# Stick-breaking attention from cumulated weights and differences of neighbouring value rows

## The chip, the cores and the metric

The kernel runs on one core of one Trainium2 chip. The metric is the device time of one execution, in microseconds (us). A core has five engines with a queue of instructions each: TensorE (PE in the profile; PEld is its loading of weights), VectorE (DVE), ScalarE (ACT), GpSimd (POOL) and SyncE (SP), which here only issues DMAs. Each engine works its queue in order and waits where an instruction's inputs are not there yet. DMAs move data between the device memory (HBM) and the on-chip memory (SBUF, 128 partitions), or within SBUF; their packets run on 16 DMA engines of the core.

## The reference

One sequence of 512 positions with 1024 features goes through two layers, all in float32. Layer 0 is gated linear attention and an MLP. Layer 1 is stick-breaking attention with 16 heads of 64 features, and an MLP; its keys and values come from one projection. The part that the change touches:

```python
z = jnp.einsum('bqhd,bkhd->bhqk', q_blk, k_blk) * scale
mask = s_idx[None, :] < t_idx[:, None]
log_1m = jnp.where(mask, jax.nn.log_sigmoid(-z), 0.0)
rev = lax.cumsum(log_1m, axis=3, reverse=True)
log_w = jax.nn.log_sigmoid(z) + (rev - log_1m)
w = jnp.where(mask, jnp.exp(log_w), 0.0)
outs.append(jnp.einsum('bhqk,bkhd->bqhd', w, v_blk))
```

So a query t gives key s < t the weight sigmoid(z_ts) times the product of (1 - sigmoid(z_tj)) over all keys j between s and t.

## The kernel before, in words

Everything is float32; most matmuls are made of three products of operands that are split into a high and a low part (`split_tile`, lines 67 to 73: ACT makes `hi`, DVE makes `lo`). The order in which each engine runs its instructions is set when the kernel is built: a scheduler orders them from the code's order, and `tc.keep_in_program_order` and `tc.high_priority` bind some of them. Buffers come from rotating pools, and an instruction that reuses a buffer waits until its last reader is done.

The stages are: gated linear attention; MLP 0; the values of layer 1 (`values`, lines 768 to 854, a product of 512x1024 by 1024x1024 made from seven half products); attention; the output projection; MLP 1.

**Values.** The last steps of the layer norm before this stage are transposes of the four 128-row tiles of the hidden state (`turn_affine`, line 231, on PE). Two of these tiles, tiles 2 and 3, are turned between the value matmuls: `late.pop(0)(None)` in lines 809 and 813 stands once after the first `part` (12 matmuls of line 794) and once later. The values end in two tiles `vs[0]` and `vs[1]`, 128 partitions x 4 blocks x 512 floats: row 128 j + p of the values is partition p of block j, and `vs[0]` holds heads 0 to 7, `vs[1]` heads 8 to 15.

**Attention** goes over eight pairs of heads, p = 0 to 7 (line 997). For each p the code does the keys and queries of pair p + 2, in the middle of which the weights of pair p are transposed (`turn`, line 962, on PE, copied out by ACT in line 967); then `weights` of pair p + 1, which begins with its scores (line 925, on PE); then `outputs` of pair p (line 976), 4 steps over the blocks of value rows. The keys are split by `put` (lines 98 and 99: `kh` on ACT, `kl` on DVE), the queries in lines 913 and 914 (`qh`, `ql`). PSUM has 8 banks that are handed out in turn, so the scores of a pair take over a bank that `kl` of the pair after next has to have read.

`weights` handles the two heads in five tiles of 128 x 512 that hold, side by side, the score rows of the blocks of queries: a mask is added on DVE (line 942); ACT makes `r` = sigmoid(-z) and `w` = sigmoid(z) (lines 949 and 950); DVE makes the running product of `r` from the right with one scan over the tile (line 952), in which a tile of zeros and ones, `begin`, restarts it where a segment ends; and the weight is `w` times the scan one column further right (line 953), on POOL for four of the five tiles and on DVE for the fifth.

Weights in device memory reach SBUF through SP's queue: `split_piece` (line 64) loads 512 KB into one of three `raw` buffers, so a load waits on SP until `split_tile` has split the piece three loads earlier, and every DMA behind it on SP's queue waits too. After p = 0 and p = 1 the code has DVE apply the layer norm's gain and bias to a tile of the hidden state (`affine`, line 196, four instructions).

Of the kernel before, what the change touches and what calls it, by code (L numbers as in the profile page):

```python
# [8 lines left out]
F32 = mybir.dt.float32  # L9
F32R = mybir.dt.float32r  # L10
I32 = mybir.dt.int32
AF = mybir.ActivationFunctionType
ALU = mybir.AluOpType

P = 128
S = 512
D = 1024
NT = S // P
# [16 lines left out]
def yoco_kernel(ctx: ExitStack, tc: tile.TileContext, x, gla_w_in, gla_w_a2, gla_b_a, gla_norm_g,  # L35
                gla_w_o, kv_w, sb_w_q, sb_w_o, mlp_w_up, mlp_w_down, ln_g, ln_b, out):
    nc = tc.nc
# [10 lines left out]
    def nm(s):  # L48
        uid[0] += 1
        return f"{s}{uid[0]}"  # L50
# [407 lines left out]
    for u in range(2):  # L458
        for t in range(NT):
            nc.sync.dma_start(out=xs[t][:, 512 * u:512 * u + 512],  # L460
                              in_=x2[128 * t:128 * t + 128, 512 * u:512 * u + 512])
# [4 lines left out]
            k = 4 * u + t  # L466
# [24 lines left out]
    for k in range(8):  # L491
# [6 lines left out]
                                   op1=ALU.subtract)  # L498
    pcs = pieces_512(w_in, 0, 8, 2 * QK + 512)
    for h in range(GH):  # L500
# [3 lines left out]
        c = slice(128 * h, 128 * h + 128)  # L504
# [153 lines left out]
    op = tc.tile_pool(name="gated", bufs=1, reuse_waits="tile")  # L658
# [21 lines left out]
    hs = [Rows() for _ in range(NT)]  # L680
    for t in range(NT):
        nc.sync.dma_start(out=hs[t].h, in_=x2[128 * t:128 * t + 128, :])
    vec, vcols = lnvec(0, 0), lncols(0, 0)
    steps = seven(*onT, lambda k, h, j: block(gla_w_o[0], 512 * k + 256 * h, 512 * j), opp, hs, True, norms=range(NT),
                  mid=lambda: turn_gated(3, 1), ends=True, begun=begun)
    hT = Split()
    late = finish(steps, vcols, hs, hT, sgs)
# [60 lines left out]
    vs = []  # L748
# [19 lines left out]
    def values(y, late, bs):  # L768

        a11, a21, a12, a22 = y[0][:, :, 0:256], y[0][:, :, 256:512], y[1][:, :, 0:256], y[1][:, :, 256:512]  # L770
        whole = lambda u, c0: lambda k, s: tuple(w[u][:, k, c0 + 128 * s:c0 + 128 * s + 128] for w in (h2T.hi, h2T.lo))
        tt = nc.vector.tensor_tensor

        def pieces(bs, keep=lambda ins: ins):
            got = []
            for b in bs:
                hi, lo = split_tile(b, 2, keep)
                got += [(hi[:, i, :], lo[:, i, :]) for i in range(2)]
            return got

        def plain(k, j):
            got = []
            for h in range(2):
                hi, lo = split_piece(v_weights(k, h, j), 2)
                got += [(hi[:, i, :], lo[:, i, :]) for i in range(2)]
            return got

        def part(s, a, b, banks, opens=True, closes=True):

            if opens:  # L790
                banks[s] = bank()
            for k in range(4):
                for x, w in ((0, 0), (0, 1), (1, 0)):
                    nc.tensor.matmul(banks[s], lhsT=a(k, s)[x], rhs=b[k][w],  # L794
                                     start=opens and (k, x, w) == (0, 0, 0),
                                     stop=closes and (k, x, w) == (3, 1, 0), skip_group_check=True)

        def fresh(s, banks, i, j):
            nc.scalar.activation(vs[j][:, 2 * i + s, :], banks[s], AF.Copy, scale=-1.0 if j else 1.0)

        def add(s, banks, i, j):
            v = vs[j][:, 2 * i + s, :]
            tt(v, v, banks[s], op=ALU.subtract if j else ALU.add)

        ys, xs, ws, zs = ([None, None] for _ in range(4))
        b21, b22, b11, b12 = bs
        p1, p2 = plain(0, 0), pieces(b21)
        part(0, whole(0, 0), p1, ys, True, False)
        late.pop(0)(None)
        part(1, whole(0, 0), p1, ys, True, False)  # L810
        part(0, whole(1, 0), p2, xs)
        keys0 = piece_128(kv_w, 0)
        late.pop(0)(None)
        part(1, whole(1, 0), p2, xs)
        more(b12, 0, 0)
        held = [bank(), bank()]
        cols_by(held[0], keys0, 0, 256)
        cols_by(held[0], keys0, 256, 256)
        queries0 = piece_128(sb_w_q[0], 0)
        cols_by(held[1], queries0, 0, 512)  # L820
        for h in range(2):
            tc.keep_in_program_order(tt(b11[h], b22[h], b11[h], op=ALU.add))
            tc.keep_in_program_order(tt(b21[h], b21[h], b11[h], op=ALU.add))
        p4 = pieces(b21, tc.keep_in_program_order)
        vs.extend([unit(F32), unit(F32)])
        tt(a22, a22, a21, op=ALU.subtract)
        p5 = split_a(a22), pieces(b12)
        for s in range(2):
            part(s, whole(1, 256), p4, ws)
        for s in range(2):  # L830
            fresh(s, ys, 0, 0)
            add(s, xs, 0, 0)
        tt(a21, a11, a21, op=ALU.subtract)
        minus = lambda out, a, b: nc.vector.scalar_tensor_tensor(out, a, -1.0, b, op0=ALU.mult, op1=ALU.subtract)
        minus(a11, a22, a11)
        p6 = split_a(a11), pieces(b11)
        for s in range(2):
            part(s, *p5, zs, True, False)
            fresh(s, ws, 1, 0)
            fresh(s, zs, 1, 1)  # L840
        minus(a12, a12, a11)
        p3 = split_a(a12), plain(1, 1)
        for s in range(2):
            part(s, *p6, ys, False, False)
            fresh(s, ys, 0, 1)
        p7 = split_a(a21), pieces(b22)
        for s in range(2):
            part(s, *p3, zs, False, True)
            add(s, zs, 0, 1)
        for s in range(2):  # L850
            part(s, *p7, ys, False, True)
            add(s, ys, 1, 1)
            add(s, ys, 1, 0)
        return held
# [24 lines left out]
    sbp = sbx.__enter__()  # L879
# [3 lines left out]

    low = tri(sbp, "low", F32, 0.0, -1.0e30, [[-1, P]], ALU.is_gt, 1)

    begin = sbp.tile([P, 6 * P], F32, name="begin")
    nc.gpsimd.memset(begin, 0.0)
    nc.gpsimd.memset(begin[:, 511:512], 1.0)
    begins = (begin[:, 0:512], begin[:, 128:640], begin[:, 256:768])

    def chain():
        return sbp.tile([P, S], F32, tag="w", bufs=6, name=nm("w"))

    HALVES = ((A0, A1), (A1, A0))

    class Pair:
# [5 lines left out]
        def part(self, tag):  # L902
            return sbp.tile([P, S], F32R, tag=tag, bufs=2, name=nm(tag))
# [26 lines left out]
        def weights(self):  # L930

            self.ws = []
            zs = self.scores()
            for kind, segs, banks in ((0, ((0, 3, 0),), (0,)), (0, ((1, 3, 0),), (1,)), (1, ((0, 2, 0), (0, 0, 384)), (2,)),
                                      (1, ((1, 2, 0), (1, 0, 384)), (3,)), (2, ((0, 1, 0), (1, 1, 256)), (4, 5))):
                n = S // len(banks)
                views = [(slice(n * i, n * i + n), zs[b][:, n * i:n * i + n]) for i, b in enumerate(banks)]

                for _, z in views:
                    z4 = z.rearrange("p (b c) -> p b c", c=P)  # L940
                    last = z4[:, (slice(3, 4), slice(2, 4), slice(1, 2))[kind], :]
                    nc.vector.tensor_tensor(last, last, low.unsqueeze(1).broadcast_to([P, last.shape[1], P]),
                                            op=ALU.add)
                r = sbp.tile([P, S + 1], F32, tag="r", bufs=3, name=nm("r"))
                w = chain()
                nc.gpsimd.memset(r[:, S:S + 1], 1.0)
                rb = r[:, 0:S]
                for at, z in views:
                    nc.scalar.activation(rb[:, at], z, AF.Sigmoid, scale=-1.0)  # L949
                    nc.scalar.activation(w[:, at], z, AF.Sigmoid)  # L950
                down = rb[:, ::-1]
                nc.vector.tensor_tensor_scan(down, down, begins[kind][:, ::-1], 1.0, op0=ALU.mult, op1=ALU.max)  # L952
                (nc.vector if kind == 2 else nc.gpsimd).tensor_tensor(w, w, r[:, 1:S + 1], op=ALU.mult)  # L953
                self.ws.append((segs, w))

        def turn(self):

# [31 lines left out]
    vec, vcols = lnvec(0, 1), lncols(1, 0)  # L989
# [3 lines left out]
        h.affine(vec, tc.keep_in_program_order)  # L993
    pairs[1].keys()
    pairs[0].weights()
    pairs[1].queries()
    for p in range(NP):
        if p + 2 < NP:
            pairs[p + 2].keys()
            made = pairs[p].turn()  # L1000
            pairs[p + 2].queries(lambda k: [next(made, None) for _ in range(TAKE.get(k, 0))])
        else:
            n = p - (NP - 2)
            pcs = pieces_512(sb_w_o[0], 0, 4, 512 * n)
            made = pairs[p].turn()
            for t in range(NT):
                hs[t].add(n, rows(oA, t, pcs, range(4)), True)
                for _ in range(((0, 1, 2, 2), (1, 1, 2, 1))[n][t]):
                    next(made, None)
        if p + 1 < NP:  # L1010
            pairs[p + 1].weights()
        if p < 2:
            hs[2 + p].affine(vec, tc.keep_in_program_order)
        if p in (4, 6):
            u = unit(F32R)
            parts += [(u[:, i, :], u[:, 2 + i, :]) for i in range(2)]
        pairs[p].outputs(*parts[p], LAST if p == NP - 1 else [(j, j, NT) for j in range(NT)])
# [88 lines left out]
```

## Time and profile before

| | us |
|---|---|
| median of 3 runs | 1117.32 |
| fastest run | 1117.02 |
| the profiled execution | 1117.43 |
| its span, first instruction to last | 1115.7 |
| PE busy in it | 1106.8 (99%) |
| DVE busy | 828.4 (74%) |
| ACT busy | 559.7 (50%) |
| POOL busy | 175.1 (16%) |

The span is what the profile's pages and times refer to; 1.7 us of the execution lie around it. An engine that is busy most of the span does not set the time by that alone: what matters is whose waiting ends last in a stage. A row of the list of groups gives line, engine, operation, output and inputs, shape and count, then the busy time and the mean duration. A row of the timeline gives start, duration and what the instruction is, and in brackets how long its engine was idle before it and which engine and line ended that.

### The profile page before, as it was taken

Reading aid. Unit: us, or ns where it says so; the run is one execution under the profiler, and the core shown is the slowest. Engines: PE = TensorE matmul, PEld = TensorE weight load, DVE = VectorE, ACT = ScalarE, POOL = GpSimd, SP = SyncE. Lnnn points to the kernel's source line nnn. Section 1 sums busy time; section 2 is a strip of 40 time slices with the busy share of each in tenths; the row PEclk is TensorE's granted clock in tenths of the full one; section 3 lists DMA queues with packets and bytes.
Section 4 is the critical chain, followed back from the end, with each engine's and each line's share of the span. In section 5 each row is a group of like instructions: output and inputs, shape, how many; then the busy total and the mean of one; then the engine's idle time right before and its main releaser. Section 6 shows DMA issues by size and latency. Waiting matters only on the chain.

```text
span 1115.7 us, 14408 instructions
## 1 busy us (share of the span) xinstructions
PE 1106.8 (99%) x5515; PEld 917.2 (82%) x5515; DVE 828.4 (74%) x993; ACT 559.7 (50%) x839; POOL 175.1 (16%) x217
## 2 busy tenths in 40 slices
PE   9999999999999999999999999999999999999998
PEld 7888888898888888888788777778988888888886
DVE  4677639957966856858899898887389767667677
ACT  4455437653533534536675666665445435336363
POOL 1011222200100100122301324330200000001132
PEclk9999999999999999999999999999999999999999
DMA  8441399392670770797743331211946816706774
GB/s 249 122 133 57 105 262 211 126 299 95 188 207 21 202 208 22 197 203 151 226 91 113 95 114 43 72 42 55 292 112 196 240 47 169 227 19 189 170 132 94
DMA packets 107544, 161.72 MB, mean 145 GB/s; under 512 B 12434, under 2 KB 37394, under 8 KB 107476
## 3 DMA queue, kind: packets, MB, share of 16 engines
q1 hardware_dynamic: 85684, 118.34, 32.6%
q0 software_dynamic: 19328, 37.75, 19.7%
q10 hardware_dynamic: 2464, 4.72, 1.2%
q8 instruction: 43, 0.70, 0.2%
q14 instruction: 25, 0.20, 0.1%
HBM read 157.64 MB, written 3.15 MB: 144 GB/s over the span
## 4 chain that ended last, share of the span: by engine, by line
PE 96%; DVE 2%; issue 1%; POOL 0%; ACT 0%; POOLq 0%; DVEq 0%; ACTq 0%
PE ps L355 29%; PE ps L93 19%; PE ps L94 19%; PE ps L95 19%; PE ps L794 3%; PE ps L976 2%; PE ps L925 2%; PE ps L962 2%; PE ps L231 1%; DVE lo L72 1%; PE ps L584 0%; DVE h L169 0%; PE ps L121 0%; DVE bst L177 0%; DVE T L99 0%
## 5 line engine op out<-in xcount | busy, mean ns | idle before, releaser
L355 PE MATMUL ps<-hi,T 128*128 128x512 f32 x1008 | 313.4, 390 | 0.1
L93 PE MATMUL ps<-T,hi 128*128 128x512 f32 (+1 forms) x776 | 290.3, 374 | 0.0
L94 PE MATMUL ps<-T,hi 128*128 128x512 f32 (+1 forms) x776 | 287.2, 370 | 0.1
L95 PE MATMUL ps<-T,lo 128*128 128x512 f32 (+1 forms) x776 | 287.0, 370 | 0.0
L72 DVE TENSOR_TENSOR lo<-raw,hi 128x1024 fp32r<-128x1024 f32 x130 | 158.5, 1224 | 98.5 <-ACT hi L70 94.8
L355 PEld LDWEIGHTS ps<-hi,T 128*128 128x128 f32 x1008 | 188.9, 188 | 40.1 <-DVE T L99 0.6
L70 ACT ACTIVATE hi<-raw 128x1024 fp32r<-128x1024 f32 x130 | 137.8, 1064 | 163.2 <-PE ps L355 58.8
L70 ACT ACTIVATE hi<-B 128x1024 fp32r<-128x1024 f32 x118 | 124.4, 1059 | 169.7 <-PE ps L94 104.0
L72 DVE TENSOR_TENSOR lo<-B,hi 128x1024 fp32r<-128x1024 f32 x118 | 142.9, 1221 | 83.9 <-ACT hi L70 83.8
L355 PE MATMUL ps<-lo,T 128*128 128x512 f32 x504 | 196.2, 389 | 0.0
L95 PEld LDWEIGHTS ps<-T,lo 128*128 128x128 f32 x776 | 146.3, 189 | 25.0
L93 PEld LDWEIGHTS ps<-T,hi 128*128 128x128 f32 x776 | 146.2, 189 | 24.3 <-issue 0.7
L94 PEld LDWEIGHTS ps<-T,hi 128*128 128x128 f32 x776 | 146.4, 189 | 23.8 <-DVE T L99 0.4
L314 POOL DMA_DIRECT2D B<-in_mlp_w_down_dram x52 | 62.9, 1257 | 544.0 <-DMA B<-in_mlp_w_down_dram 378.5
L355 PEld LDWEIGHTS ps<-lo,T 128*128 128x128 f32 x504 | 94.6, 188 | 19.5
L169 DVE TENSOR_TENSOR h<-h,ps 128x512 f32<-128x512 f32 x110 | 74.8, 682 | 6.9 <-PE ps L95 4.0
L93 PE MATMUL ps<-hi,T 128*128 128x512 f32 x192 | 77.4, 403 | 0.0
L95 PE MATMUL ps<-hi,T 128*128 128x512 f32 x192 | 75.3, 392 | 0.0
L94 PE MATMUL ps<-lo,T 128*128 128x512 f32 x192 | 75.1, 391 | 0.0
L952 DVE TENSOR_TENSOR_SCAN r<-r,begin 128x512 f32<-128x512 f32 x40 | 65.8, 1650 | 2.8 <-ACT r L949 2.8
L953 POOL TENSOR_TENSOR w<-w,r 128x512 f32<-128x512 f32 x32 | 51.9, 1624 | 94.5 <-DVE r L952 68.2
L99 DVE TENSOR_TENSOR T<-s,T 128x1024 fp32r<-128x1024 f32 (+1 forms) x50 | 53.4, 1069 | 10.6 <-ACT T L98 10.6
(190 smaller groups left out, 1243.4 us busy)
## 6 DMA issues: line engine op xcount, KB each, us to landing
raw<-in_mlp_w_up_dram SPq DMA_DIRECT2D x64, 512.0 KB, 5.6
B<-in_mlp_w_down_dram SPq DMA_DIRECT2D x64, 512.0 KB, 5.3
B<-in_mlp_w_down_dram POOLq DMA_DIRECT2D x52, 512.0 KB, 8.0
raw<-in_gla_w_in_dram SPq DMA_DIRECT2D x20, 512.0 KB, 3.6
raw<-in_mlp_w_down_dram SPq DMA_DIRECT2D x16, 512.0 KB, 4.4
B<-in_gla_w_o_dram POOLq DMA_DIRECT2D x14, 512.0 KB, 8.5
raw<-in_kv_w_dram SPq DMA_DIRECT2D x12, 512.0 KB, 4.5
B<-in_gla_w_o_dram SPq DMA_DIRECT2D x8, 512.0 KB, 6.2
```

Of the source, the lines that this page charges most:

```text
L70: keep(nc.scalar.activation(hi, raw, AF.Copy))
L72: keep(nc.vector.tensor_tensor(lo, raw, hi.bitcast(F32), op=ALU.subtract))
L93: keep(nc.tensor.matmul(ps, lhsT=a[0], rhs=b[0], start=first, stop=False))
L94: keep(nc.tensor.matmul(ps, lhsT=a[0], rhs=b[1], start=False, stop=False))
L95: keep(nc.tensor.matmul(ps, lhsT=a[1], rhs=b[0], start=False, stop=last))
L99: keep(nc.vector.tensor_tensor(lo, ps, hi.bitcast(F32), op=ALU.subtract))
L169: nc.vector.tensor_tensor(h, h, ps, op=op)
L314: nc.gpsimd.dma_start(out=b.rearrange("p (a b) -> p a b", a=2), in_=weights(k, h, j), accum_op=ALU.add)
L355: nc.tensor.matmul(banks[s], lhsT=a(k, s)[x], rhs=b[k][y], start=opens and (k, x, y) == (0, 0, 0), stop=closes and (k, x, y) == (3, 1, 0), ...
L794: nc.tensor.matmul(banks[s], lhsT=a(k, s)[x], rhs=b[k][w], start=opens and (k, x, w) == (0, 0, 0), stop=closes and (k, x, w) == (3, 1, 0), ...
L952: nc.vector.tensor_tensor_scan(down, down, begins[kind][:, ::-1], 1.0, op0=ALU.mult, op1=ALU.max)
L953: (nc.vector if kind == 2 else nc.gpsimd).tensor_tensor(w, w, r[:, 1:S + 1], op=ALU.mult)
```

## The change

Let c_s be the sum of the weights of keys s and later. Then c_s = sigmoid(z_s) + (1 - sigmoid(z_s)) c_(s+1), and the sum of w_s v_s over s equals the sum of c_s (v_s - v_(s-1)), with v_(-1) = 0. The change computes c with one scan (multiply by `r`, add sigmoid(z)) where there was a scan and a product, and takes differences of neighbouring value rows. A scan restarts where it begins, so tiles with two segments get two scans.

The difference of rows needs, on partition p, the row of partition p - 1. `differences(n)` copies each of the four blocks of `vs[n]` into a tile, shifted down by one partition: one DMA of 127 rows of 2 KB, and one of a single row from the last partition of the block before (for the first block POOL writes zeros). All of these are issued on SP's queue. Then four subtractions on DVE overwrite `vs[n]`. `differences(0)` stands after the first `weights`; `differences(1)` after the `weights` in iteration p = 1. The two `affine` calls of that loop move from p = 0 and 1 to p = 1 and 2. The tile for c has 9 buffers where `w` had 6.

The other edit is to the order of two tiles in `values`: tile 2 is now turned in the middle of the second `part`, after 6 of its 12 matmuls, instead of before it.

```diff
-        def part(s, a, b, banks, opens=True, closes=True):
+        def part(s, a, b, banks, opens=True, closes=True, mid=None):
...
             for k in range(4):
+                if mid and k == 2:
+                    mid()
...
         part(0, whole(0, 0), p1, ys, True, False)
-        late.pop(0)(None)
-        part(1, whole(0, 0), p1, ys, True, False)
+        part(1, whole(0, 0), p1, ys, True, False, lambda: late.pop(0)(None))
...
     def chain():
-        return sbp.tile([P, S], F32, tag="w", bufs=6, name=nm("w"))
+        return sbp.tile([P, S], F32, tag="c", bufs=9, name=nm("c"))
+
+    def differences(n):
+
+        v, shifted = vs[n], [chain() for _ in range(NT)]
+        for t in range(NT):
+            if t == 0:
+                nc.gpsimd.memset(shifted[t][0:1, :], 0.0)
+            else:
+                nc.sync.dma_start(out=shifted[t][0:1, :], in_=v[P - 1:P, t - 1, :])
+            nc.sync.dma_start(out=shifted[t][1:P, :], in_=v[0:P - 1, t, :])
+        for t in range(NT):
+            nc.vector.tensor_tensor(v[:, t, :], v[:, t, :], shifted[t], op=ALU.subtract)
...
-                nc.gpsimd.memset(r[:, S:S + 1], 1.0)
-                rb = r[:, 0:S]
+                r, c = sbp.tile([P, S], F32, tag="r", bufs=3, name=nm("r")), chain()
                 for at, z in views:
...
-                down = rb[:, ::-1]
-                nc.vector.tensor_tensor_scan(down, down, begins[kind][:, ::-1], 1.0, op0=ALU.mult, op1=ALU.max)
-                (nc.vector if kind == 2 else nc.gpsimd).tensor_tensor(w, w, r[:, 1:S + 1], op=ALU.mult)
-                self.ws.append((segs, w))
+                for at in ((slice(0, S),), (slice(0, 3 * P), slice(3 * P, S)), (slice(0, 2 * P), slice(2 * P, S)))[kind]:
+                    down = c[:, at][:, ::-1]
+                    nc.vector.tensor_tensor_scan(down, r[:, at][:, ::-1], down, 0.0, op0=ALU.mult, op1=ALU.add)
+                self.ws.append((segs, c))
...
     pairs[0].weights()
+    differences(0)
     pairs[1].queries()
...
-        if p < 2:
-            hs[2 + p].affine(vec, tc.keep_in_program_order)
+        if p == 1:
+            differences(1)
+        if p in (1, 2):
+            hs[1 + p].affine(vec, tc.keep_in_program_order)
```

Three places of the built order, since the scheduler decides where the new instructions stand. In these rows `T_4805` is `vs[0]` and `T_4806` is `vs[1]`; `raw` are the loads of weights, three buffers in turn.

First, SP's queue at the first group of copies. Before, load followed load there:

```order
L64 DMA raw_5601<-in_sb_w_q_dram 128x8x128
L64 DMA raw_5755<-in_kv_w_dram 128x8x128
L64 DMA raw_5790<-in_sb_w_q_dram 128x8x128
L64 DMA raw_5944<-in_kv_w_dram 128x8x128
L64 DMA raw_5979<-in_sb_w_q_dram 128x8x128
```

Now seven copies stand behind the same load of keys:

```order
L64 DMA raw_5605<-in_sb_w_q_dram 128x8x128
L64 DMA raw_5756<-in_kv_w_dram 128x8x128
L898 DMA c_5135<-T_4805 127x512
L897 DMA c_5136<-T_4805 1x16x32
L898 DMA c_5136<-T_4805 127x512
L897 DMA c_5137<-T_4805 1x16x32
L898 DMA c_5137<-T_4805 127x512
L897 DMA c_5138<-T_4805 1x16x32
L898 DMA c_5138<-T_4805 127x512
L64 DMA raw_5791<-in_sb_w_q_dram 128x8x128
L64 DMA raw_5938<-in_kv_w_dram 128x8x128
```

The copies are issued when that load is, and the loads after it come behind them. The single row is written as 16 pieces of 32 floats, the 127 rows are left whole. The second group, of `T_4806`, stands in the same form six loads further on, behind the first load of `sb_w_o`.

Second, DVE behind the weights of pair 0. Before, the last rows of that `weights`, then the splitting of pieces, queries and keys:

```order
L953 TENSOR_TENSOR w_5137<-w_5137,r_5136 128x512
L72 TENSOR_TENSOR lo_5570<-raw_5566,hi_5568 128x1024
L72 TENSOR_TENSOR lo_5605<-raw_5601,hi_5603 128x1024
L914 SCALAR_TENSOR_TENSOR ql_5177<-ps_5151,qh_5176 128x512
L72 TENSOR_TENSOR lo_5759<-raw_5755,hi_5757 128x1024
L99 TENSOR_TENSOR kl_5212<-ps_5186,kh_5211 128x512
L72 TENSOR_TENSOR lo_5794<-raw_5790,hi_5792 128x1024
L914 SCALAR_TENSOR_TENSOR ql_5282<-ps_5221,qh_5281 128x512
```

Now:

```order
L72 TENSOR_TENSOR lo_5574<-raw_5570,hi_5572 128x1024
L72 TENSOR_TENSOR lo_5609<-raw_5605,hi_5607 128x1024
L900 TENSOR_TENSOR T_4805<-T_4805,c_5135 128x512
L922 SCALAR_TENSOR_TENSOR ql_5183<-ps_5157,qh_5182 128x512
L900 TENSOR_TENSOR T_4805<-T_4805,c_5136 128x512
L900 TENSOR_TENSOR T_4805<-T_4805,c_5137 128x512
L900 TENSOR_TENSOR T_4805<-T_4805,c_5138 128x512
L72 TENSOR_TENSOR lo_5760<-raw_5756,hi_5758 128x1024
L99 TENSOR_TENSOR kl_5218<-ps_5192,kh_5217 128x512
L72 TENSOR_TENSOR lo_5795<-raw_5791,hi_5793 128x1024
L922 SCALAR_TENSOR_TENSOR ql_5288<-ps_5227,qh_5287 128x512
```

The four subtractions, each of which waits for its copy, stand ahead of everything that DVE does for pairs 1 and 2, except `ql` of pair 1, which stands behind the first.

Third, DVE behind the weights of pair 2. Before:

```order
L196 TENSOR_TENSOR h_1640<-h_1640,lng_5013 128x512 x2
L196 TENSOR_TENSOR h_1640<-h_1640,lnb_5014 128x512 x2
L99 TENSOR_TENSOR T_5012<-ps_5555,T_5011 128x512
L72 TENSOR_TENSOR lo_6138<-raw_6134,hi_6136 128x1024
L99 TENSOR_TENSOR kl_5598<-ps_5572,kh_5597 128x512
L72 TENSOR_TENSOR lo_6173<-raw_6169,hi_6171 128x1024
```

Now:

```order
L99 TENSOR_TENSOR T_5009<-ps_5559,T_5008 128x512
L900 TENSOR_TENSOR T_4806<-T_4806,c_5539 128x512
L900 TENSOR_TENSOR T_4806<-T_4806,c_5540 128x512
L72 TENSOR_TENSOR lo_6125<-raw_6121,hi_6123 128x1024
L900 TENSOR_TENSOR T_4806<-T_4806,c_5541 128x512
L900 TENSOR_TENSOR T_4806<-T_4806,c_5542 128x512
L196 TENSOR_TENSOR h_1639<-h_1639,lng_5010 128x512 x2
L196 TENSOR_TENSOR h_1639<-h_1639,lnb_5011 128x512 x2
L99 TENSOR_TENSOR kl_5602<-ps_5576,kh_5601 128x512
L72 TENSOR_TENSOR lo_6160<-raw_6156,hi_6158 128x1024
```

The `kl` at the end is that of pair 4, whose bank the scores of pair 3 take over; the second group of subtractions now stands ahead of it.

More of the change, by code (lines that the diff above doesn't have):

```diff
@@ L884, in yoco_kernel @@
     low = tri(sbp, "low", F32, 0.0, -1.0e30, [[-1, P]], ALU.is_gt, 1)
[L886 to L889, printed above, removed]
     def chain():
-        return sbp.tile([P, S], F32, tag="w", bufs=6, name=nm("w"))
+        return sbp.tile([P, S], F32, tag="c", bufs=9, name=nm("c"))
[9 more added lines that the diff above has]
+            nc.vector.tensor_tensor(v[:, t, :], v[:, t, :], shifted[t], op=ALU.subtract)
     HALVES = ((A0, A1), (A1, A0))
@@ L943, in weights @@
                                             op=ALU.add)
-                r = sbp.tile([P, S + 1], F32, tag="r", bufs=3, name=nm("r"))
-                w = chain()
-                nc.gpsimd.memset(r[:, S:S + 1], 1.0)
-                rb = r[:, 0:S]
+                r, c = sbp.tile([P, S], F32, tag="r", bufs=3, name=nm("r")), chain()
                 for at, z in views:
-                    nc.scalar.activation(rb[:, at], z, AF.Sigmoid, scale=-1.0)
-                    nc.scalar.activation(w[:, at], z, AF.Sigmoid)
-                down = rb[:, ::-1]
-                nc.vector.tensor_tensor_scan(down, down, begins[kind][:, ::-1], 1.0, op0=ALU.mult, op1=ALU.max)
-                (nc.vector if kind == 2 else nc.gpsimd).tensor_tensor(w, w, r[:, 1:S + 1], op=ALU.mult)
-                self.ws.append((segs, w))
+                    nc.scalar.activation(r[:, at], z, AF.Sigmoid, scale=-1.0)
+                    nc.scalar.activation(c[:, at], z, AF.Sigmoid)
+                for at in ((slice(0, S),), (slice(0, 3 * P), slice(3 * P, S)), (slice(0, 2 * P), slice(2 * P, S)))[kind]:
+                    down = c[:, at][:, ::-1]
+                    nc.vector.tensor_tensor_scan(down, r[:, at][:, ::-1], down, 0.0, op0=ALU.mult, op1=ALU.add)
+                self.ws.append((segs, c))
         def turn(self):
```

## The prediction, made before the changed kernel was run

> **What bounds the kernel now.** I read the page first, then who waited for whom, then stretches of the attention stage.
>
> ```profile
> PE 1106.8 (99%) x5515; PEld 917.2 (82%) x5515; DVE 828.4 (74%) x993; ACT 559.7 (50%) x839; POOL 175.1 (16%) x217
> PE 96%; DVE 2%; issue 1%; POOL 0%; ACT 0%; POOLq 0%; DVEq 0%; ACTq 0%
> PE ps L231 <- DVE h L190: 1.2, 2, 1.0
> PE ps L925 <- DVE kl L99: 0.5, 1, 0.5
> 646.00:656.00 10.00, 10.00 (x52) 7.37 (x51) 9.67 (x12) 7.26 (x15) 6.26 (x7) 1.00 0.19 57
> 656.00:664.00 8.00, 8.00 (x62) 6.67 (x62) 6.94 (x10) 4.50 (x10) 0.65 (x3) 1.00 0.41 128
> ```
>
> PE is busy 1106.8 of 1115.7 us and carries 96% of the chain that ends last. In attention (the last two rows: stretch, then busy time of PE, PEld, DVE, ACT, POOL, then clock, DMA share and GB/s) PE has no gap at all. So whatever DVE and POOL save there is worth nothing unless PE waits for them, and PE's recorded waits after the start are 1.2 and 0.5 us. The change leaves PE's matmuls as they are. Its gain is at most those 1.7 us; what it can lose is open upwards: every new wait of PE counts in full.
>
> **The tile order: -1.0 us.**
>
> ```profile
> 549.83 1.09 PE L231 MATMUL ps<-ident,h 128*128 128x128 f32 x8 [1.03 <-DVE h L190]
> 548.97 0.81 DVE L190 TENSOR_SCALAR h<-h,mv,rs 128x1024 f32<-128x1024 f32 x1 [0.16 <-POOL rs L184]
> ```
>
> Before its transposes PE stood 1.03 us for DVE's centring, which ends at 549.78. With six matmuls (0.227 us apart, 1.36 us) in between, PE arrives later than that, so the gap goes. Tile 3 and everything behind it then run 1.0 earlier on PE, ACT and DVE alike.
>
> **Scans and products: 0 to -0.5 us.**
>
> ```profile
> 606.62 1.23 DVE L952 TENSOR_TENSOR_SCAN r<-r,begin 128x512 f32<-128x512 f32 x1 [0.60 <-ACT r L949]
> 608.07 2.12 DVE L952 TENSOR_TENSOR_SCAN r<-r,begin 128x512 f32<-128x512 f32 x1
> 610.82 1.68 DVE L72 TENSOR_TENSOR lo<-raw,hi 128x1024 fp32r<-128x1024 f32 x1
> 608.02 1.09 POOL L953 TENSOR_TENSOR w<-w,r 128x512 f32<-128x512 f32 x1 [17.03 <-ACT w L950]
> L952 DVE TENSOR_TENSOR_SCAN r<-r,begin 128x512 f32<-128x512 f32 x40 | 65.8, 1650 | 2.8 <-ACT r L949 2.8
> 656.93 1.28 DVE L196 TENSOR_TENSOR h<-h,lng 128x512 f32<-128x512 f32 x2
> 643.96 0.50 PE L925 MATMUL ps<-kh,qh 64*128 64x512 f32 x1 [0.51 <-DVE kl L99]
> ```
>
> A scan takes 1.23 us alone and 2.12 beside POOL's multiplication. Without it 40 tiles cost 40 x 1.23 = 49 us where they cost 65.8. A scan in two parts adds one instruction's fixed part, 24 times, between nothing and 0.1 us each; I take 2 us in all. Eight products on DVE go (about 1.3 us each, 10) and eight subtractions come (about 0.68 each by the `affine` row, 5.5). DVE saves some 20 us, POOL over 50, and PE hides nearly all of it. Only the 0.51 us at 643.96, where `kl` came late behind the `affine` of p = 0, can go.
>
> **The copies.** No row shows a copy within SBUF or one of 127 rows. The near end is a load of 128 rows, 512 KB in 3.8 us to landing. The far end is that a copy gets one of the 16 DMA engines alone.
>
> ```profile
> raw<-in_kv_w_dram SPq DMA_DIRECT2D x5, 512.0 KB, 3.8
> DMA packets 15277, 13.81 MB, mean 77 GB/s; under 512 B 416, under 2 KB 11680, under 8 KB 15264
> q1 hardware_dynamic: 15264, 13.63, 24.5%
> ...
> DMA packets 107544, 161.72 MB, mean 145 GB/s; under 512 B 12434, under 2 KB 37394, under 8 KB 107476
> gcol<-in_ln_g_dram SPq DMA_DIRECT2D x3, 4.0 KB, 11.2
> bcol<-in_ln_b_dram SPq DMA_DIRECT2D x3, 4.0 KB, 7.9
> wa_raw<-in_gla_w_in_dram SPq DMA_DIRECT2D x1, 64.0 KB, 5.2
> a<-in_gla_b_a_dram SPq DMA_DIRECT2D x2, 2.0 KB
> 7.00:12.00 5.00, 5.00 (x26) 3.64 (x25) 2.58 (x4) 2.52 (x5) 0.00 (x0) 1.00 1.05 403
> ```
>
> The first three rows are for 590 to 770 us, where only loads of 128 rows run, in packets of 512 B and more: the 416 smaller ones are 26 x 16, as if each DMA ended with one small packet on each of 16 engines. In the whole span 12434 are small. Six vectors in pieces of 4 B are 6 x 1024, the 64 KB in pieces of 64 B are 1024, which leaves 5266. The DMA view lists 331 DMAs; 331 x 16 would be 5296, and 5266 is 329 x 16 + 2: two DMAs seem to end with one packet instead of 16. The two one-row loads of 2 KB are the likely ones, as all others have 16 rows or more. So the number of engines follows the rows. If it is the largest number that divides them, 127, a prime, gives 1; if rows are rounded up, 16. The single-row copies are written as 1x16x32 in the built order, as one would for the dividing rule, and the 127 rows are left whole. I take one engine.
>
> The Trainium skill ("DMA: Bandwidth & Descriptors", section "Why a DMA increments its semaphore by 16 and not by 1") states the dividing rule for DMAs issued from SP, names 127 partitions as a case of one engine, and says that it is always the lowest-numbered one. The count of small packets agrees for one row; no run here shows 127.
>
> One engine at its best: 403 GB/s / 16 = 25.2 GB/s, so 127 x 2048 B take 10.3 us. At its attention-stage rate: 13.63 MB over 24.5% of 16 x 180 us is 19.3 GB/s, 13.5 us. I take 10.3, since one engine's packets queue back to back, as in the full stretch. Four copies in one queue take 41.2 us.
>
> *Group 1.*
>
> ```profile
> 612.53 0.37 SPq L64 DMA_DIRECT2D raw<-in_kv_w_dram  x1
> 627.26 2.37 PE L976 MATMUL ps<-wt,T 128*64 128x512 f32 x16
> 638.50 1.09 ACT L967 ACTIVATE wt<-ps 128x512 f32<-128x512 f32 x2 [0.67 <-PE ps L962]
> 659.94 1.20 DVE L72 TENSOR_TENSOR lo<-raw,hi 128x1024 fp32r<-128x1024 f32 x1
> 661.07 0.67 DVE L99 TENSOR_TENSOR kl<-ps,kh 128x512 fp32r<-128x512 f32 x1
> out_dram<-h SPq DMA_DIRECT2D x2, 128.0 KB, 2.2
> ```
>
> The load ahead of the copies goes out when DVE has split an older piece: at 612.53, and now about 2.0 earlier (1.0 from the tile order, 0.9 + 0.5 as the rows of 2.12 and 1.68 shrink to 1.22, less 0.4 because the first scan also needs the second sigmoid), 610.5. The first copy waits 0.4 for its issue, 1.3 for the load's own sixteenth (32 KB) on the engine, and some 1.5 of fixed time (128 KB land in 2.2 us, of which 0.3 is moving at 403 GB/s and 0.4 issue). So the fourth lands at 610.5 + 0.4 + 1.3 + 1.5 + 41.2 = 654.9; subtraction 0.7, the last step of `outputs` 0.3: 655.9. Before, these outputs ended at 629.6. **+26.3 us**, the 1.0 of the tile order included. DVE stands at the subtractions meanwhile, and behind them in its queue are two splits, `kl` and `ql` (by the steps of such rows 1.1 + 0.6 + 1.1 + 0.6 = 3.5 us) and the weights of pair 1; the load of queries behind the copies and its `hi` add about 2. PE has some 8.2 us of keys and queries before the transposes of those weights (ACT copied the first out at 638.50). Their second tile comes, with 4.6 for masks, sigmoids and two scans, some 10 us after the last subtraction: 2 us of waiting, and by estimate 1 more at the scores. **+3.1**, less the 0.5 that stood there before.
>
> *Group 2.* In the old trace the load ahead of it was issued at 645.24, 0.8 before the scores of pair 2 ended (646.07). Those scores now end at 646.07 + 26.3 + 3.1 - 0.5 = 675.0.
>
> ```profile
> 645.24 0.37 SPq L64 DMA_DIRECT2D raw<-in_sb_w_o_dram  x1
> 646.07 2.37 PE L976 MATMUL ps<-wt,T 128*64 128x512 f32 x16
> 661.77 0.53 PE L925 MATMUL ps<-kh,qh 64*128 64x512 f32 x2
> ```
>
> Copies: 674.2 + 0.4 + 1.3 + 1.5 + 41.2 = 718.6; subtraction 0.7, the two pairs of `affine` rows 2.4, `kl` of pair 4 0.7: 722.4. Only then can PE begin the scores of pair 3, which began at 661.77. PE's own work in between is 15.7 us (646.07 to 661.77 before) and ends near 691. **The total is +60.6.** From there on DVE has less to do than before and nothing is late.
>
> *Clock.*
>
> ```profile
> 1.57 2.18 PE L451 MATMUL ps<-ident 128*128 128x128 f32 x9 [1.57 <-POOL ident L132]
> 620.04 1.03 PE L962 MATMUL ps<-ident,w 128*128 128x128 f32 x8
> 1113.00:1114.00 1.00, 0.00 (x0) 0.00 (x0) 0.00 (x0) 0.00 (x0) 0.00 (x0) 0.60 1.04 374
> 1114.00:1115.70 1.70, 0.00 (x0) 0.00 (x0) 0.00 (x0) 0.00 (x0) 0.00 (x0) 0.50 0.01 3
> ```
>
> The granted clock falls to half some 3 us after the last matmul, and at the start 9 transposes took 2.18 us where later 8 take about 0.9; that lasted to about 7 us, 5.5 us at half speed, a loss of 2.7. Each long wait will end so. The first loss hides under the 3.1 above, the second adds **+2.7**. The Trainium skill ("TensorE: Matmul & The Clock Gate", section "What's actually happening") puts the warm-up at about 3.4 us of sustained work; by it the loss would be 1.7, and the sum 1 us less.
>
> **Sum.** The profiled execution took 1117.43 us, 0.1 above the median of 1117.32. 1117.43 + 60.6 + 2.7 = 1180.7; I say **1180**. Slow copies (13.5 us) give 8 x 3.2 = 26 more, 1206; without restart, fixed times and cold clock it is about 9 less, 1171; packets that overlap better than in any row, 10% faster, a further 8 less.
>
> **Rivals.** (a) *Not slower: the copies are spread over 16 engines.* It decides at one point, whether 127 rows divide. Then a group of four lands within some 8 us of its issue, near 619, when DVE gets there; PE needs it from 626. Group 2 would land before DVE's scans are done, and `kl` of pair 4, 15 us of DVE work behind the queries, still meets PE. Both old gaps go: 1117.43 - 1.03 - 0.51 = 1115.9. For it speaks that every load with 128 rows is spread; against it the 5266 packets. (b) *One engine per copy, but another one each time.* Each copy lands 11.8 us after its issue: group 1 by 625.8, at most 0.5 late; group 2 some 4 us behind DVE's scans, 2 on PE: about 1118.5. (c) *The change does not do what it says:* the tile order could leave the gap, if centring were later still. The rows say it is not; 1 us, inside every case.
>
> **Chances.** One engine 0.82, spread 0.12, one each 0.06. The first alone is 8 in 10, so the range is its own: from 1158 (the 1171 less the 8 and some for the estimate of the restarts) to 1212 (the slow copies and 6 for restarts). A change of 2% (22.3 us) is about what a measurement of this kernel can tell from none. All of the first case lies above 1139.7: slower 0.82, same 0.17, faster 0.01, as PE's 1106.8 us of matmuls leave no room for 22 us less.
>
> **What the profile would show.** The copies: landing in some 12, 22, 32, 43 us after issue, and small packets that grow by less than 16 per DMA. PE: a wait at line 976 on DVE line 900 of some 26 us, one at line 925 on `kl` of some 30, and a clock near 0.5 after each. DVE: idle before line 900, for DMAs. Scans without rows of 2.1 us; PE's gap at line 231 gone. I am wrong if the copies land in 4 us (then 1116), or if a lone engine moves packets far faster or slower than 81 to 107 ns each.

## The result, and the profile after

The changed kernel takes **1184.55 us** (median of 4 runs, 1183.17 to 1185.64) where the kernel before took 1117.17 beside it: a ratio of 1.0598, 95% interval 1.0584 to 1.0611 (the quotient of the two medians is 1.0603). It is slower by 67.4 us. One of the four executions of the kernel before took 1856.85 us, and the median of the other three is 1117.02. The forecast was 1180, with a range of 1158 to 1212. The profiled execution took 1185.64 us, its span is 1183.9.

The page of the changed kernel: busy times, the row of PE in forty slices with the granted clock below it (in tenths of full speed), the DMA packets, and the shares of the chain of waits.

```profile
PE 1112.1 (94%) x5515; PEld 920.1 (78%) x5515; DVE 806.7 (68%) x1017; ACT 559.4 (47%) x839; POOL 120.1 (10%) x145
PE   9999999999999999999991753999999999999998
PEclk9999999999999999999996785999999999999999
DMA packets 108760, 163.81 MB, mean 138 GB/s; under 512 B 12634, under 2 KB 37594, under 8 KB 108692
PE 89%; DVE 3%; DMA 3%; SPq 3%; issue 1%; ACT 1%; POOL 0%; POOLq 0%; DVEq 0%; ACTq 0%
```

DVE lost 21.7 us of work and POOL 55.0, and the kernel is slower all the same: PE's row has a hole in slices 22 to 25, and the chain that ends last now leads through DMAs and SP's queue. The small packets grew from 12434 by 200. That is 6 x 16 pieces of 128 B of the single rows, 6 x 16 closing packets of these rows, and 8: each of the eight copies of 127 rows closes with one packet, where 16 engines would have made 128.

Who waited for whom on PE (engine and line, what it waited for; total, times, longest):

```profile
PE ps L933 <- DVE kl L99: 62.1, 2, 31.1
PE ps L933 <- DVE ql L922: 2.2, 1, 2.2
PE ps L451 <- POOL ident L132: 1.6, 1, 1.6
PE ps L231 <- DVE h L190: 0.2, 1, 0.2
```

Two waits of 31 us in the scores (line 933) are nearly all of the loss. The gap at line 231 has shrunk to 0.2. The timeline of PE around the first wait, then of DVE and ACT:

```profile
626.26 0.50 PE L933 MATMUL ps<-kh,qh 64*128 64x512 f32 x1 [2.19 <-DVE ql L922]
657.75 0.79 PE L933 MATMUL ps<-kh,qh 64*128 64x512 f32 x1 [30.98 <-DVE kl L99]
661.57 3.07 PE L981 MATMUL ps<-wt,T 128*64 128x512 f32 x16
```

```profile
624.92 0.69 DVE L900 TENSOR_TENSOR T<-T,c 128x512 f32<-128x512 f32 x1 [8.71 <-DMA c<-T]
635.09 0.69 DVE L900 TENSOR_TENSOR T<-T,c 128x512 f32<-128x512 f32 x1 [8.88 <-DMA c<-T]
645.18 0.69 DVE L900 TENSOR_TENSOR T<-T,c 128x512 f32<-128x512 f32 x1 [9.39 <-DMA c<-T]
655.26 0.69 DVE L900 TENSOR_TENSOR T<-T,c 128x512 f32<-128x512 f32 x1 [9.39 <-DMA c<-T]
655.87 1.22 DVE L72 TENSOR_TENSOR lo<-raw,hi 128x1024 fp32r<-128x1024 f32 x1
657.01 0.69 DVE L99 TENSOR_TENSOR kl<-ps,kh 128x512 fp32r<-128x512 f32 x1
656.76 1.06 ACT L70 ACTIVATE hi<-raw 128x1024 fp32r<-128x1024 f32 x1 [32.70 <-DMA raw<-in_sb_w_q_dram]
```

The copies land 10.1 us apart and DVE stands for each. Behind the last subtraction come a split and `kl`, and 0.74 us after `kl` begins PE goes on. In those 31 us PE had only one of the two heads' first scores begun: the bank for the other was the one that `kl` had yet to read. ACT stood too, for a load of weights. SP's queue, its issues by start and duration, shows why that load was late:

```profile
610.47 0.37 SPq L64 DMA_DIRECT2D raw<-in_kv_w_dram  x1
611.00 0.72 SPq L898 DMA_DIRECT2D c<-T  x1
611.77 4.58 SPq L897 DMA_DIRECT2D c<-T  x1
616.39 0.63 SPq L898 DMA_DIRECT2D c<-T  x1
617.07 9.31 SPq L897 DMA_DIRECT2D c<-T  x1
626.42 0.61 SPq L898 DMA_DIRECT2D c<-T  x1
627.08 9.33 SPq L897 DMA_DIRECT2D c<-T  x1
636.44 0.61 SPq L898 DMA_DIRECT2D c<-T  x1
637.16 9.26 SPq L64 DMA_DIRECT2D raw<-in_sb_w_q_dram  x1
```

An issue behind a long copy stands 9.3 us on SP: the row ahead of the third copy until 626.38, 1.5 us after DVE got the first copy, the one ahead of the fourth until 636.41, 1.3 after the second. Stretches of the two waits and behind them (length, busy time of PE, PEld, DVE, ACT, POOL, granted clock, DMA share, GB/s):

```profile
632.00:640.00 8.00, 0.00 (x0) 0.00 (x0) 0.69 (x1) 0.00 (x0) 0.00 (x0) 0.50 0.07 26
662.00:663.00 1.00, 1.00 (x4) 0.24 (x2) 1.00 (x3) 1.00 (x4) 0.00 (x0) 0.50 0.52 156
663.00:664.00 1.00, 1.00 (x8) 0.42 (x6) 1.00 (x2) 1.00 (x3) 0.00 (x0) 1.00 0.00 0
734.00:735.00 1.00, 1.00 (x5) 0.75 (x4) 1.00 (x3) 1.00 (x5) 0.00 (x0) 0.66 0.00 0
```

During the wait a sixteenth of the DMA engines' time is used and 26 GB/s move: one engine of 16. The clock is at half then, and stays there until 663.0, 5.2 us after PE's restart; after the second wait (restart at 728.64) until some 734.7, 6.0 us (0.66 in the last row is a third of the microsecond at full speed).

### The profile page after: what moved, and what is told of

It reads as the page before. It is cut to its first block, busy times and chain, and to the rows that moved or that the text cites. A ratio compares the mean times of both kernels' runs of the same rounds, so it can differ in the third digit from the quotient of the medians.

```text
span 1183.9 us, 14352 instructions
## 1 busy us (share of the span) xinstructions
PE 1112.1 (94%) x5515; PEld 920.1 (78%) x5515; DVE 806.7 (68%) x1017; ACT 559.4 (47%) x839; POOL 120.1 (10%) x145
## 4 chain that ended last, share of the span: by engine, by line
PE 89%; DVE 3%; DMA 3%; SPq 3%; issue 1%; ACT 1%; POOL 0%; POOLq 0%; DVEq 0%; ACTq 0%
PE ps L355 28%; PE ps L93 17%; PE ps L94 17%; PE ps L95 17%; DMA c<-T 3%; SPq L897 3%; PE ps L796 2%; PE ps L981 2%; PE ps L933 1%; PE ps L967 1%; DVE lo L72 1%; PE ps L231 1%; DVE h L196 1%; PE ps L584 0%; PE ps L121 0%
## 5 line engine op out<-in xcount | busy, mean ns | idle before, releaser
L933 PE MATMUL ps<-kh,qh 64*128 64x512 f32 (+3 forms) x64 | 13.8, 371 | 64.3 <-DVE kl L99 62.1
L933 PEld LDWEIGHTS ps<-kh,qh 64*128 64x128 f32 x64 | 8.0, 203 | 67.9 <-DVE kl L99 62.6
```

What stands on the lines that cost most here:

```text
L933: nc.tensor.matmul(zs[b + a][:, at], lhsT=self.q[x][own, P * i:P * i + P], rhs=self.k[y][own, 0:n], start=(x + y == 0), stop=(x == 1), ski ...
```

## The experiments

**The copies cut to spread, and the parts without them.** Four kernels run together, beside 1117.21 for the kernel before. Before them my theory was: the number of engines that a copy gets is the largest number up to 16 that divides its rows, and DVE's standing for the copies is the loss.

First, each copy in two, of 112 and 15 rows:

```diff
-            nc.sync.dma_start(out=shifted[t][1:P, :], in_=v[0:P - 1, t, :])
+            nc.sync.dma_start(out=shifted[t][1:113, :], in_=v[0:112, t, :])
+            nc.sync.dma_start(out=shifted[t][113:P, :], in_=v[112:P - 1, t, :])
```

> Each copy of 127 rows is written as one of 112 rows (16 x 7) and one of 15. Theory (the rows are divided evenly over engines, and 127 leaves one engine): 7 packets of 2 KB per engine and copy, 0.6 us by the 81 ns of a packet, and some 2 us to landing; twelve issues on SP of 0.4 to 0.7 us. The first group lands near 620, before PE needs the differences at 626; both long waits of PE at line 933 go: 1115.9 us, 1115 to 1118. Rival (copies within SBUF are slow as such, or the order of the subtractions ahead of kl on DVE costs): a large part of the 67 us stays, 1150 or more.

Measured: **1115.16 us**, ratio 0.998 (0.9972 to 0.9989). The same bytes, by more DMAs, and the 69 us are gone. Its DMA issues (count, KB each, median us from issue to landing) and DVE's last subtraction of the first group:

```profile
c<-T SPq DMA_DIRECT2D x8, 224.0 KB, 3.1
c<-T SPq DMA_DIRECT2D x8, 30.0 KB, 2.4
621.36 0.69 DVE L901 TENSOR_TENSOR T<-T,c 128x512 f32<-128x512 f32 x1 [1.10 <-DMA c<-T]
```

So a copy within SBUF is not slow as such, and the subtractions ahead of `kl` cost PE nothing.

Second, the kernel before with the other tile order alone (the edit to `part` in the diff of the change, nothing else):

> The kernel before with the tile order alone. Theory: PE's 1.03 us at line 231 go and nothing takes their place, -1.0 us, 1116.2. Rival: the gap moves to a later tile or a later stage, 1117.2.

Measured: 1115.72 us, ratio 0.9988 (0.9979 to 0.9997). PE's wait at line 231 is 0.2 us and the one for `kl` is still there:

```profile
PE ps L926 <- DVE kl L99: 0.5, 1, 0.5
PE ps L231 <- DVE h L190: 0.2, 1, 0.2
```

Third, the changed kernel without both groups of differences:

```diff
-    differences(0)
...
-        if p == 1:
-            differences(1)
```

> The changed kernel without both differences (no copies, no subtractions; so the values are weighted by the cumulated weights as they are): scans and tile order alone. Theory: the arithmetic is hidden by PE and all of the loss is in the differences: 1115.9 us, 1115 to 1117. Rival: part of the loss is the longer way from the sigmoids to the weights, or the moved affine: over 1120.

Measured: 1115.09 us, ratio 0.9983 (0.9974 to 0.9992). Against 1115.72 for the tile order alone, scans and products are worth 0.6 us by the medians, no more than the measurement can tell. All of the loss is in the differences.

Fourth, two engines instead of one:

```diff
-            nc.sync.dma_start(out=shifted[t][1:P, :], in_=v[0:P - 1, t, :])
+            nc.sync.dma_start(out=shifted[t][1:123, :], in_=v[0:122, t, :])
+            nc.sync.dma_start(out=shifted[t][123:P, :], in_=v[122:P - 1, t, :])
```

> Each copy as one of 122 rows (2 x 61) and one of 5. Theory (divided evenly): two engines, 61 packets of 2 KB each, 4.9 us a copy, 20 us a group. The waits of PE were 31 us with copies 10.1 us apart, so 9.4 us of four copies lie beside PE's work; 4 x 4.9 - 9.4 = 10 us per group, and some 5 for restart and clock: 1141 us, 1133 to 1147. Rival (any number but a prime is spread over 16): 1116. Rival (what costs is not the copies' length): 1175 or more.

Measured: **1139.72 us**, ratio 1.0203 (1.0189 to 1.0217), 1.3 below the forecast. The two first subtractions are 4.91 us apart (10.17 with 127 rows):

```profile
620.91 0.69 DVE L901 TENSOR_TENSOR T<-T,c 128x512 f32<-128x512 f32 x1 [4.32 <-DMA c<-T]
625.82 0.69 DVE L901 TENSOR_TENSOR T<-T,c 128x512 f32<-128x512 f32 x1 [4.22 <-DMA c<-T]
```

Half of the bytes per engine is half of the time per copy, with the same number of bytes in all. The dividing rule holds for a number that is no prime. The small packets say the same. Without the 192 of the single rows they grow by 56 here (12682 in all), which is 8 x (2 + 5): the 122 rows close with two packets and the 5 rows with five. With 112 and 15 rows they grow by 248 (12874), which is 8 x (16 + 15).

**Four engines.** Run later, beside 1117.83:

```diff
-            nc.sync.dma_start(out=shifted[t][1:P, :], in_=v[0:P - 1, t, :])
+            nc.sync.dma_start(out=shifted[t][1:125, :], in_=v[0:124, t, :])
+            nc.sync.dma_start(out=shifted[t][125:P, :], in_=v[124:P - 1, t, :])
```

> Each copy as one of 124 rows (4 x 31) and one of 3. Theory (divided evenly): four engines, 31 packets of 2 KB each, 2.5 us a copy; 4 x 2.5 - 9.4 = 0.6 us of waiting per group and hardly a cold clock: 1116.5, 1115 to 1119. With 127 rows (31.1 a group) and 122 (10) it makes a straight line in the packets per engine, 127, 61 and 31, that meets zero at about 29. Rival (the loss goes with the number of DMAs or the order on DVE): 1125 or more.

Measured: 1118.98 us, ratio 1.0009 (1.0000 to 1.0019), at the upper edge of what was expected. PE waited 2.8 us for `ql` and 1.0 for `kl`, 1.9 per group, where the line gave 0.6: it bends near zero rather than meeting it. Per group (half of a kernel's waits for `kl` and `ql`) PE waits 32.2, 9.7 and 1.9 us at 127, 61 and 31 packets per engine. The small packets are again 12682, so 56 = 8 x (4 + 3).

**One group at a time.** Two kernels, beside 1117.25. In the first, `differences(1)` is left out, in the second `differences(0)`.

> The changed kernel with the first group of differences alone (copies of 127 rows left whole; the values of heads 8 to 15 stay undifferenced). Theory (each group stops PE for itself): 1115.1 without differences, and of the 62.1 + 2.2 us of waits of the changed kernel 31 + 2.2, and some 2 of a cold clock: 1150, 1146 to 1153. Rival (the first group delays the loads behind it and these make the second wait): 1165 or more here, and under 1140 with the second group alone.

> The changed kernel with the second group of differences alone (the values of heads 0 to 7 stay undifferenced). Theory (each group stops PE for itself): 1115.1 + 31.1 + some 2 of a cold clock: 1149, 1145 to 1153; the two costs, of the first group alone and of the second alone, add up to the 69 us of both. Rival: under 1140.

Measured: 1151.35 (ratio 1.0301, 1.0284 to 1.0319) and 1149.11 (1.0281, 1.0266 to 1.0297). Over 1115.09 that is 36.3 and 34.0; the sum, 70.3, is near the 69.5 of both groups together. Each group stops PE for itself; the first does not make the second's wait. PE's waits and busy time in the first kernel, and its wait in the second:

```profile
PE ps L933 <- DVE kl L99: 31.0, 1, 31.0
PE 1109.1 (96%) x5515; PEld 917.8 (80%) x5515; DVE 803.6 (70%) x1013; ACT 559.4 (49%) x839; POOL 119.5 (10%) x144
```

```profile
PE ps L933 <- DVE kl L99: 31.2, 1, 31.2
```

PE's busy time holds the price of the cold clock, since the matmuls are the same: 1105.2 us without differences, 1109.1 with the first group, 1108.3 with the second, 1112.1 with both. That is some 3.5 us per long wait. It is a rough price: kernels without a long wait have between 1105.0 and 1106.8 us in the same figure.

**The copies without the subtractions.** Eight instructions of DVE are left out, the copies stay:

```diff
-        for t in range(NT):
-            nc.vector.tensor_tensor(v[:, t, :], v[:, t, :], shifted[t], op=ALU.subtract)
```

> All copies as in the changed kernel, without the eight subtractions (nothing reads the copied tiles before they are overwritten). DVE no longer stands for the copies, but SP's queue does, some 9.3 us at each issue behind a long copy, and the loads behind come some 18 us later (the load of queries was issued at 637 where it went out at 619 before). Theory (DVE's stand, with kl behind it, is the whole loss): 1115 to 1118. Rival (the late loads cost too): 1120 to 1150, by what PE then waits for ACT's hi or DVE's lo.

Measured: **1167.35 us**, ratio 1.0447 (1.0431 to 1.0462). Here my theory fell: without any stand of DVE for a copy, 52 of the 69 us are still there, and more than my rival's upper end. PE's first wait and what ACT waited for:

```profile
659.36 0.80 PE L93 MATMUL ps<-T,hi 128*128 128x512 f32 x1 [31.62 <-DVE ql L920]
656.39 1.06 ACT L70 ACTIVATE hi<-raw 128x1024 fp32r<-128x1024 f32 x1 [33.08 <-DMA raw<-in_sb_w_q_dram]
721.43 0.60 ACT L953 ACTIVATE c<-ps 128x512 f32<-128x512 f32 x1 [9.15 <-DMA c<-T]
```

The load of queries that was issued at 636.78, behind the fourth copy, is there at 656.4. ACT stands at its `hi`, DVE at its `lo`, and `ql` of an older pair, which frees the bank that PE wants next, stands behind that `lo`. PE waits 31.6 us, the same as before, by another way. So two paths of almost one length lead through the first group of copies: over the last subtraction (655.26 in the changed kernel) and over the load (656.76 there). Taking the subtractions away gains next to nothing in this group; the load's path is taken away further down.

The rest is another 14.0 us of PE in the second group, which belongs to this experiment alone: nothing reads the copied tiles now, so the sigmoids of a later pair that reuse these buffers are the first to wait for the copies (the third row), and the cold clock: PE is busy 1111.6 us where it was 1105.2 without differences.

**The load out of the way.** To see the subtractions' path alone in the first group, from the kernel with that group alone:

```diff
-    def split_piece(src, a):
+    def split_piece(src, a, queue=nc.sync):
...
-        nc.sync.dma_start(out=raw.rearrange("p (a b) -> p a b", a=a), in_=src)
+        queue.dma_start(out=raw.rearrange("p (a b) -> p a b", a=a), in_=src)
...
-            ps = ps or cols(h2T, piece_128(kv_w, P * self.p))
+            ps = ps or cols(h2T, piece_128(kv_w, P * self.p, nc.gpsimd if self.p >= 4 else nc.sync))
...
-            ps = ps or cols(h2T, piece_128(sb_w_q[0], P * self.p), mid)
+            ps = ps or cols(h2T, piece_128(sb_w_q[0], P * self.p, nc.gpsimd if self.p >= 3 else nc.sync), mid)
```

> The kernel with the first group of differences alone (1151.4; the values of heads 8 to 15 stay undifferenced), but the loads of weights that stood behind the copies (queries from pair 3 on, keys from pair 4 on) go out on POOL's queue, so no load stands behind a copy. Theory (two paths of nearly the same length lead through the copies: the subtractions with kl behind them on DVE, and the load of queries with ACT's hi behind the last copy on SP; either alone stops PE some 31 us): PE still waits some 31 us for kl at line 933, 1148 to 1151. Rival (the late load is what decides, the subtractions only look so): under 1140.

Measured: 1140.58 us, ratio 1.0205 (1.0184 to 1.0227): between the two expectations. The reason is not in either: with fewer loads ahead of them on SP, the first copy went out 16 us earlier and the last one 7 us earlier, and the copies took longer, as it seems because of the other loads on the engines between them. (The profiled execution is the longest of the four, 1144.62 us; in it PE also stands 2.3 us at line 231, ahead of this stage.)

```profile
595.29 0.72 SPq L898 DMA_DIRECT2D c<-T  x1
647.91 0.69 DVE L900 TENSOR_TENSOR T<-T,c 128x512 f32<-128x512 f32 x1 [9.28 <-DMA c<-T]
650.39 0.79 PE L933 MATMUL ps<-kh,qh 64*128 64x512 f32 x1 [21.95 <-DVE kl L99]
```

PE still waits for `kl`, 22.0 us, and goes on 2.48 us after the last subtraction begins; in the changed kernel it was 2.49. The subtraction is 7.35 us earlier and so is PE. No load was late (ACT's waits for loads in this stage are under 4 us). So this path stops PE by itself as well. How long it would with the copies at 611 was not measured; by the 2.49 us an estimate is the 31 us of the changed kernel.

**Another queue.** The copies of 127 rows whole, but issued by POOL:

```diff
-            nc.sync.dma_start(out=shifted[t][1:P, :], in_=v[0:P - 1, t, :])
+            nc.gpsimd.dma_start(out=shifted[t][1:P, :], in_=v[0:P - 1, t, :])
```

> The copies of 127 rows issued by POOL's queue instead of SP's; the single rows stay on SP. Theory that the shape alone sets the number of engines: still some 10 us a copy and 40 a group, 1175 to 1185, but loads on SP no longer stand. Rival (the number of engines is a matter of how SP's DMAs are cut up): POOL's copies use all 16, land in a few us, no wait of PE: 1115 to 1118.

Measured: **1115.21 us**, ratio 0.9983 (0.9973 to 0.9992). The shape alone does not decide. From POOL the same 127 rows land in 2.9 us:

```profile
c<-T POOLq DMA_DIRECT2D x8, 254.0 KB, 2.9
638.19 0.53 POOL L898 DMA_DIRECT2D c<-T  x1
PE 1105.0 (99%) x5515; PEld 915.3 (82%) x5515; DVE 805.4 (72%) x1017; ACT 559.1 (50%) x839; POOL 124.6 (11%) x153
```

254 KB in 2.9 us is 90 GB/s, more than three engines at the 26 GB/s of one. Most of that time is not spent moving: while one of these copies ran with no load beside it, 238 GB/s moved and the DMA engines were busy 88%.

```profile
597.50:598.50 1.00, 1.00 (x6) 0.84 (x5) 1.00 (x2) 0.00 (x0) 0.00 (x0) 1.00 0.88 238
```

The small packets grow by 320 over the kernel before (12754 in all), 192 of the single rows and 8 x 16. Both agree with copies that are spread over all 16 engines. One DMA costs POOL 0.53 us or a little more, and POOL has the time since the products have left it. The first group also went out earlier, from 585.8, as no load stands ahead of it there; the second at 638 to 641, where SP's went out at 644 to 670 in the kernel with that group alone. The 6 us by which the first of them starts earlier are far less than the 31 us that go, so it is mainly the landing that removes them. The Trainium skill ("DMA: Bandwidth & Descriptors", section "Why a DMA increments its semaphore by 16 and not by 1") says that some direct copies issued from GpSimd use all 16 engines, with the rows rounded up, 127 among its examples; the 2.9 us agree with it.

This kernel and the one with 112 and 15 rows beat the kernel before by 2.0 us (0.2%), and the changed one by 69. Of the 2.0 us the tile order alone gives 1.5, so what the cumulated weights themselves gain can't be told from nothing.

## Why the prediction was right, step by step

- **The bound** held within the measurement. With the copies out of the way the change gives 1115.2 us, against 1115.9 for the rival in which they were spread; the gain is 2.0 us (interval 1.2 to 3.1 with 112 and 15 rows), where the bound was 1.7. DVE's and POOL's savings are worth nothing visible.
- **Tile order, -1.0:** the trace shows 1.0 less at line 231, the timing 1.5 less with an interval of 0.3 to 2.3. **Scans and products, 0 to -0.5:** 0.6 measured, not told from nothing. The 64 scans cost 48.3 us where 51 were reckoned, and DVE's saving is 21.7 where 20 were.
- **One engine, 10.3 us a copy:** 10.1 measured. This was the step that decided. The 5266 small packets showed it for copies of one row before any copy of 127 had run; that 127 rows would go the same way was argued, from the dividing rule and the way the single rows are written, and the 8 closing packets and the 26 GB/s of the changed kernel bear it out. The first was there 13.9 us after its issue, by DVE's start, instead of 12.
- **Group 1 was mis-sized.** The prediction had +28.9 net; the first group alone cost 34.1 over the kernel before. The place was wrong: I let the scores of pair 1 pass and put the stop at the outputs behind them. In fact PE stopped inside these scores, since their second bank waited for `kl` of pair 2, which stands behind the subtractions. So their 3.8 us and the whole outputs came after the stop, and the outputs ended at 664.6 instead of 655.9; the 2.6 us of the cold clock are part of these 8.7. In return the waits at the transposes and scores behind (+3.1) did not come. The rule was in my own description of the kernel, that a pair's scores take over a bank that `kl` of the pair after next has to have read; I had applied it to group 2 alone.
- **Group 2, 31.7 of waiting and 2.7 of clock:** 34.4 predicted, 34.0 measured with this group alone. The wait was 31.1 us in the changed kernel, for `kl` of pair 4 as forecast, but PE did not stand before all of these scores: it ran three quarters of them first (695.75 to 697.53) and stood at the rest. It also came to them some 1 us sooner behind the load's issue than reckoned (15.5 us instead of 16.5). The two errors have opposite signs, so a little of the close agreement is luck.
- **Clock:** 2.7 was right in size for one wait (half of 5.2 and 6.0 by the windows, 3 to 4 by PE's busy time), but the first was not hidden under a later wait, as there was none. It was counted once and came twice. The 2.7 came from the durations at the start of the program; the rows of the clock read 1.00 there, so only the waits show the half clock directly. By the 3.4 us of the Trainium skill ("TensorE: Matmul & The Clock Gate", section "What's actually happening") the loss would be an estimated 1.7. These runs show no one time: after the first wait the clock stayed at half for 5.2 us in the changed kernel, for 6.4 with the first group alone (657.74 to some 664.2) and for 3.3 with 122 and 5 rows (632.63 to 635.9), each time with the same scores behind it. What sets it within this range stays open.
- **SP's issues at 0.4 us** were wrong by a factor of twenty, as they stood 9.3 us. It did not change when the copies landed, since they follow at 10.1 us without a gap: the one DMA engine was the limit anyway. The load of queries "adds about 2" was right as a date (1.5 after the last subtraction) and incomplete as a cause: alone it is a second stop of 31 us.

Of the rivals, (b), another engine each time, is excluded by copies that follow at 10.1 us and by 26 GB/s in the wait, though two copies were under way at a time (the second was issued at 616.39 and there at 635.09, 18.7 us later instead of 11.8); (c) by line 231; (a) is what POOL's queue does.

## What to carry to other kernels

Look at the number of rows of every DMA, not only at its bytes: on SP's queue 127 rows ran on one engine and 122 on two, and 112 + 15 cost PE no wait. For DMAs on SP's queue the small packets of a profile tell how many engines each used, one packet for each engine. A slow DMA stops what is queued behind it in two places, on the engine that waits for its data and on the queue that issues the loads behind it; where taking away one wait gains nothing, look for a second path of the same length. And follow an engine's wait through the banks: here it was what stood behind the waiting subtraction, `kl`, that stopped PE, sooner than the differences themselves.

## What the runs showed of the hardware that was not expected

- An issue on SP behind copies of 127 packets on one engine stands 9.3 us, and some 4.5 behind the first copy of a group; with 61 packets per engine 2.2 to 4.8 us, and with copies of 112 and 15 rows at most 0.9. What limits it, packets or DMAs in flight, was not tried.
- The same copy from POOL's queue lands in 2.9 us instead of 10 or more, and its eight copies close with 128 small packets instead of 8.
- The clock stayed at half for 3.3 to 6.4 us after PE's restart from a long wait: 5.2 and 6.0 us in the changed kernel, 6.4 with the first group alone, 3.3 and 4.8 with 122 and 5 rows, 3.9 without the subtractions. Neither the kind of matmul behind the wait (3.3, 5.2 and 6.4 are the same scores) nor the length of the wait (3.9 and 5.2 follow waits of 31 us) orders these numbers.
